# Three of the four weight sums of a Strassen pair made by accumulating DMAs instead of VectorE

## The chip, the cores and the metric

The kernel runs on one core of a Trainium2 chip. The metric is the device time of one execution in microseconds (us). The runs shown are 2701.43, 2702.08 and 2699.49 us (median 2701.43); besides them one execution was recorded by the profiler. Engines are named as the profile names them: PE is TensorE, DVE is VectorE, ACT is ScalarE, POOL is GpSimd, SP is SyncE. All DMAs of the kernel before are issued by SP.

## The reference

Two layers of one trunk work on 512 latent and 256 context tokens of width 2048, in float32. Each layer normalises and modulates the tokens, multiplies them with one wide input matrix, runs four groups of attention heads, and multiplies the gated result with an output matrix. In the last layer the context tokens are needed only as keys and values.

```python
for l in range(DEPTH):                       # DEPTH = 2
    with_ctx = l < DEPTH - 1
    shift, scale, gate = jnp.split(silu_c @ w_mod[l] + b_mod[l], 3, axis=-1)
    n = rms_norm(h, pre_norm_g[l]) * (1.0 + scale[:, None]) + shift[:, None]
    nc = rms_norm(hc, pre_norm_g[l]) * (1.0 + scale_c) + shift_c
    p = jnp.split(n @ w_in[l], split_points, axis=-1)      # w_in[l]: 2048 x 7168
    pc = jnp.split(nc @ w_in[l], split_points, axis=-1)
    ...                                                    # four attention groups oa, ob, on, od
    y = (jnp.concatenate([oa, ob, on, od], axis=-1) * jax.nn.silu(p[12])) @ w_out[l]
    h = h + gate[:, None] * rms_norm(y, post_norm_g[l])
```

The change touches only the product with `w_in`.

## The kernel before

**Numbers as pairs.** A float32 matrix is held as a high part in `fp32r` and a low part with the rest. One product is three matmuls: high times high, high times low, low times high (`mm3`, L301 to L303). `split` makes the two parts: ACT copies the high part (L292), then DVE subtracts it from the source (L293). Split weights lie in the tiles `wh` and `wl`, four buffers each, so a split waits until PE is done with the product four before.

**The Strassen stage.** The 56 column blocks of `w_in` (128 columns each) are taken in 28 pairs per layer. For the first half of the 2048 input channels a pair is a 2 by 2 matrix of quarters (512 channels x 128 columns, 256 KB) times a 2 by 2 matrix of token blocks; it is done in seven products instead of eight. The four quarters of a pair are loaded by SP into `wr` (L211, six buffers); `g[0]` and `g[3]` are the two quarters of the first column block, `g[1]` and `g[2]` those of the second. Four sums of quarters are needed, and DVE makes all of them: L166 makes `s1 = g1 + g2`, L167 makes `s2 = s1 - g0`, L168 makes `g0 - g1` in place in `g[1]`, and L179 makes `g3 - s2` in place in `g[3]`. `s1` and `s2` lie in two buffers, tag `wsum`. The seven products run in the order 1, 6, 2, 5, 7, 3, 4 (in the first pair of a layer 1, 2, 6, 5, 7, 3, 4); product 6 takes `s2`, product 5 takes `s1`, product 7 takes the sum in `g[1]` and product 3 the sum in `g[3]`.

**Banks.** Products 1 and 2 gather in one PSUM bank, products 6, 5 and 3 in a second, products 7 and 4 in a third. After each product ACT or DVE reads its bank: 1 and 2 by ACT (L777, L781), 6, 5 and 3 by DVE with the copy `s` of product 1 (L784, `c<-ps,s`), 7 and 4 by DVE onto what stands in `c` (L784, `c<-ps,c`). PE may not go on in a bank that is not read yet: product 3 waits for the read of 5, product 4 for the read of 7. When products 3 and 4 are read, `c` is stored to `part` (L787).

**Wide and narrow.** In layer 0 every product has 384 moving columns (512 latent and 256 context tokens in two halves). In layer 1 the pairs of keys and values have 384 (12 pairs, called wide below), those of queries and gates 256 (16 pairs, narrow).

**Order.** `weight()` is called before each product and first calls `weights_ahead()`, which issues the splits up to two products ahead and all loads for which a buffer is free; the sums of a pair are issued after the split for product 3 of the pair before. During the stage the step list `late` puts columns of the modulation (`w_mod`) beside the products: loads `mraw` (L426) and DVE's L443. The order of the instructions on an engine is set when the kernel is built, by a scheduler that goes by data dependences, and each engine runs its own list strictly in that order.

**Between the layers.** `out_phase` ends layer 0 with the residual (L1442), the norm of the next layer and its transposes (`token_half`, L559), and `reload` makes the token operands of products 1 to 7 (splits into `arena`) from `token_sums` (L570 to L575). The first weight sums of layer 1 are made there too. The second half of the input channels is done later, block by block, in the attention stage, and is not touched.

Of the kernel before, what the change touches and what calls it, by code (L numbers as in the profile page):

```python
# [10 lines left out]
F32 = mybir.dt.float32  # L11
# [3 lines left out]
ALU = mybir.AluOpType  # L15
# [3 lines left out]
P = 128  # L19
# [63 lines left out]
class Kernel:  # L83
# [35 lines left out]


    def push_pair(self, l, s, b1, b2, order):
        g = {"sums": False}
        for i, (b, c) in enumerate(((b1, 2 * s), (b2, 2 * s), (b2, 2 * s + 1), (b1, 2 * s + 1))):
            self.lq.append((g, i, ("in", (l, b, c))))
        self.wq += [("st", g, n) for n in order]

    def push_one(self, kind, key):
# [25 lines left out]
    def new_pair(self):  # L153
# [2 lines left out]
        self.ws[self.wsplit] = hi, lo  # L156
        return hi, lo

    def sums(self, g):

        if g["sums"] or not all(self.need(g, i) for i in range(3)):
            return g["sums"]
        add = self.nc.vector
        g["s1"] = self.wp.tile([P, 512], F32, tag="wsum", bufs=2, name="s1")
        g["s2"] = self.wp.tile([P, 512], F32, tag="wsum", bufs=2, name="s2")
        add.tensor_add(g["s1"], g[1], g[2])  # L166
        add.tensor_sub(g["s2"], g["s1"], g[0])  # L167
        add.tensor_sub(g[1], g[0], g[1])  # L168
        g["sums"] = True
        return True  # L170

    def split_product(self, g, n):
        if not all(self.need(g, i) for i in {1: (0,), 2: (3,)}.get(n, ())) or not self.sums(g):
            return False
        src = {1: 0, 6: "s2", 2: 3, 5: "s1", 7: 1, 3: 3, 4: 2}[n]
        hi, lo = self.new_pair()
        self.split(hi, lo, g[src])
        if n == 2:
            self.nc.vector.tensor_sub(g[3], g[3], g["s2"])  # L179
        elif src in (0, 1, 2, 3):  # L180
            self.retire(g, src)
        if n == 3:
            for kind, other, m in self.wq[self.wsplit + 2:self.wsplit + 3]:
                if kind == "st":
                    self.sums(other)
        return True
# [14 lines left out]
    def load_one(self):  # L201
        nc, a = self.nc, self.a
        if self.live >= self.raws or self.wload >= len(self.lq):
            return False
        g, i, (kind, key) = self.lq[self.wload]
        if kind == "og" and key not in self.stored:
            return False
        raw = self.wp.tile([P, 512], F32, tag="wr", bufs=RAWS, name="wr")
        if kind == "in":
            l, b, c = key  # L210
            nc.sync.dma_start(raw, a["w_in"][l, b, :, 4 * c:4 * c + 4, :].rearrange("p k c -> p (k c)"))  # L211
        elif kind == "out":
            l, k, c = key
            nc.sync.dma_start(raw, a["w_out"][l, k * P:(k + 1) * P, c * 512:(c + 1) * 512])
        else:
            l, s, k = key
            w0, w = ((0, SEQ), (SEQ, CTX))[s]
            raw = raw[:, 0:w]
            nc.sync.dma_start(raw, self.ogd[l, k, :, w0:w0 + w])
        g[i] = raw  # L220
        self.live += 1
        self.wload += 1
        return True
# [227 lines left out]
    def mod_finish(self, job, accs, fold=True):  # L451

        nc = self.nc
        l, kind, c4, streams = job
        ns = len(streams)
        if not fold or ns == 1:
            ps = self.tbank()
            for j in range(4):
                for i in range(ns):
                    nc.tensor.matmul(ps[:, ns * j + i:ns * j + i + 1], accs[i][:, j * P:(j + 1) * P], self.ones[:, 0:1], start=True, stop=True)  # L460
            self.mod_columns(l, kind, c4, ps[:, 0:4 * ns].rearrange("p (j s) -> p j s", s=ns))
            return
        if ns == 2:
            t, col = self.mp.tile([P, 512], F32, tag="mt", bufs=2, name="fold"), self.halves
            a, b = slice(0, 64), slice(64, P)
            nc.scalar.activation(t[a], accs[0][b], AF.Copy)
            nc.scalar.activation(t[b], accs[1][a], AF.Copy)
            nc.vector.tensor_add(t[a], t[a], accs[0][a])
            nc.vector.tensor_add(t[b], t[b], accs[1][b])

        def sums():
            ps = self.tbank()
            for j in range(4):
                nc.tensor.matmul(ps[:, ns * j:ns * j + ns], t[:, j * P:(j + 1) * P], col, start=True, stop=True)
            self.mod_columns(l, kind, c4, ps[:, 0:4 * ns].rearrange("p (j s) -> p j s", s=ns))

        self.later(2, sums)
# [83 lines left out]
    def token_sums(self, ns, ts, what):  # L561


        add = self.nc.vector

        def step(j):
            (b11, b12), (b21, b22) = ns[j], ns[4 + j]
            x, y = ts[j]
            if what == 1:
                add.tensor_sub(x, b12, b11)  # L570
                add.tensor_sub(y, b22, x)
            elif what == 4:
                add.tensor_sub(y, b21, y)
            else:
                add.tensor_sub(x, b22, b12)  # L575

        return [lambda j=j: step(j) for j in range(4)]

    def reload(self, n, ns, ts):

        hi, lo = self.operand(n)

        def step(j):
            if n in (1, 2, 3):
                src = ns[j + (0 if n == 1 else 4)][int(n == 3)]
            else:
                src = ts[j][{5: 0, 7: 0, 6: 1, 4: 1}[n]]
            self.split(hi[:, j], lo[:, j], src)

        return [lambda j=j: step(j) for j in range(4)]  # L590

# [155 lines left out]
    def pair_slots(self, l, n, i, order, hooks=None):  # L747

        nc = self.nc
        blocks = self.units[n][3][i]  # L750
        wide = l < DEPTH - 1 or blocks[0][0] == "k"
        w = HT if wide else 2 * P
        before, after = hooks or ({}, {})
        r = {}

        def slot(m, half):
            if half == 0:
                for fn in before.get(m, ()):
                    fn()
                r["w"] = self.weight()  # L760
            hi, lo = r["w"]
            th, tl = self.operand(m)
            out = self.bank(CHAIN[m], w)
            for j in (2 * half, 2 * half + 1):
                js = slice(j * P, (j + 1) * P)
                self.anchors[1] = self.mm3(out, hi[:, js], lo[:, js], th[:, j, 0:w], tl[:, j, 0:w], m in FIRST and j == 0, m in LAST and j == 3, True)
            if half:
                read(m, out)
                for fn in after.get(m, ()):
                    fn()  # L770

        def read(m, ps):
            V = nc.vector
            if m == 1:
                r["c"] = [self.cp.tile([P, 2, HT], F32, tag="c", bufs=4, name="c")[:, :, 0:w] for _ in blocks]
                r["s"] = self.cp.tile([P, HT], F32, tag="s", bufs=1, name="s")[:, 0:w]
                nc.scalar.activation(r["s"], ps, AF.Copy)  # L777
                return
            c1, c2 = r["c"]
            if m == 2:  # L780
                nc.scalar.activation(c1[:, 0], ps, AF.Copy)  # L781
            else:
                c = {6: c2[:, 0], 4: c2[:, 0], 5: c2[:, 1], 7: c2[:, 1], 3: c1[:, 1]}[m]
                self.anchors[0] = V.tensor_add(c, ps, c if m in (7, 4) else r["s"])  # L784
            if m in (3, 4):
                c, (_, b) = (c1, blocks[0]) if m == 3 else (c2, blocks[1])
                nc.sync.dma_start(self.part[l, b, :, :, 0:w], c)  # L787

        return [lambda m=m, half=half: slot(m, half) for m in order for half in range(2)]
# [94 lines left out]
    def qk_block(self, l, b, kind, is_q, dst):  # L884
# [33 lines left out]
        def norm_part(c, sl, part):  # L918
# [31 lines left out]
            def scale(dg):  # L950
# [3 lines left out]
                self.split_to(dst, sl, x)  # L954

            self.later(4, sums)

        return done
# [654 lines left out]
```

## Time and profile before

| what | before |
|---|---|
| median of the runs | 2701.43 us |
| profiled execution, its own time | 2703.73 us |
| its span, first to last instruction | 2701.6 us |
| mean granted TensorE clock | 0.984 |
| busy: PE, DVE, ACT, POOL | 96%, 81%, 48%, 2% |
| Strassen stage of layer 0, of layer 1 | about 90 to 510 us, about 1580 to 1917 us |
| DMAs issued by POOL | none |

A line of the profile's windows gives, for a stretch of the span, the busy time of each engine with the number of its instructions in brackets, the granted clock as a share of full speed, the share of time in which the 16 DMA engines were busy, and what they moved. A line of a group of instructions ends with the busy time and the mean length in ns, and after a second bar the idle time of that engine just before these instructions, with what ended it. A timeline row gives start and length in us, engine, line, operation and tiles, and in square brackets the idle time before it. Matmuls are pipelined, so their busy time overlaps itself; the step from one to the next is read from their number in a window.

### The profile page before, as it was taken

Reading aid. Unit: us, or ns where it says so; the run is one execution under the profiler, and the core shown is the slowest. Engines: PE = TensorE matmul, PEld = TensorE weight load, DVE = VectorE, ACT = ScalarE, POOL = GpSimd, SP = SyncE. Lnnn points to the kernel's source line nnn. Section 1 sums busy time; section 2 is a strip of 40 time slices with the busy share of each in tenths; the row PEclk is TensorE's granted clock in tenths of the full one; section 3 lists DMA queues with packets and bytes.
Section 4 is the critical chain, followed back from the end, with each engine's and each line's share of the span. In section 5 each row is a group of like instructions: output and inputs, shape, how many; then the busy total and the mean of one; then the engine's idle time right before and its main releaser. Section 6 shows DMA issues by size and latency. Waiting matters only on the chain.

```text
span 2701.6 us, 41385 instructions
## 1 busy us (share of the span) xinstructions
PE 2591.7 (96%) x14392; PEld 2231.2 (83%) x14392; DVE 2187.2 (81%) x4480; ACT 1285.7 (48%) x2532; POOL 43.6 (2%) x42
## 2 busy tenths in 40 slices
PE   7899999999999999999999689999999999999997
PEld 1799999987888888887777479999878887888885
DVE  4899998789899888767889989887798988876524
ACT  3534343445556455546533464444455554544422
POOL 0000000000000000000010000000000000000001
PEclk9899999999999999999999789999999999999998
DMA  9455554422223334427886535444422334444632
GB/s 318 138 197 194 196 196 149 151 73 78 85 96 116 119 126 142 140 89 232 293 269 218 201 123 170 148 146 137 152 87 86 112 121 136 146 154 129 223 103 98
DMA packets 230497, 411.09 MB, mean 152 GB/s; under 512 B 25568, under 2 KB 59664, under 8 KB 229776
## 3 DMA queue, kind: packets, MB, share of 16 engines
q1 hardware_dynamic: 230288, 408.45, 46.3%
q8 instruction: 113, 1.85, 0.3%
q14 instruction: 96, 0.79, 0.1%
HBM read 348.17 MB, written 60.19 MB: 151 GB/s over the span
## 4 chain that ended last, share of the span: by engine, by line
PE 76%; DVE 11%; DMA 7%; ACT 3%; issue 2%; SPq 0%; POOL 0%; DVEq 0%; ACTq 0%; POOLq 0%
PE ps L301 23%; PE ps L302 23%; PE ps L303 22%; DMA mraw<-in_w_mod 3%; PE ps L1132 3%; DVE macc L443 2%; DVE wl L293 1%; PE ps L650 1%; PE ps L1034 1%; DMA mr<-in_w_mod 1%; DVE rt L862 1%; DVE h L1442 1%; PE ps L1035 1%; DMA wr<-in_w_out 1%; DMA wr<-ogd 1%
## 5 line engine op out<-in xcount | busy, mean ns | idle before, releaser
L301 PE MATMUL ps<-arena,wh 128*128 128x384 f32 (+2 forms) x3104 | 1050.6, 339 | 16.6 <-ACT arena L292 7.4
L302 PE MATMUL ps<-arena,wh 128*128 128x384 f32 (+2 forms) x3104 | 1038.8, 335 | 0.0
L303 PE MATMUL ps<-arena,wl 128*128 128x384 f32 (+2 forms) x3104 | 1037.7, 335 | 0.0
L292 ACT ACTIVATE wh<-wr 128x512 fp32r<-128x512 f32 x696 | 437.8, 630 | 710.1 <-PE ps L302 371.3
L301 PEld LDWEIGHTS ps<-arena,wh 128*128 128x128 f32 x3104 | 586.9, 189 | 47.5 <-ACT arena L292 8.6
L293 DVE TENSOR_TENSOR wl<-wr,wh 128x512 fp32r<-128x512 f32 x696 | 477.4, 688 | 176.3 <-ACT wh L292 163.7
L303 PEld LDWEIGHTS ps<-arena,wl 128*128 128x128 f32 x3104 | 587.0, 189 | 33.0
L302 PEld LDWEIGHTS ps<-arena,wh 128*128 128x128 f32 x3104 | 587.8, 189 | 27.4 <-DVE arena L293 1.1
L443 DVE SCALAR_TENSOR_TENSOR macc<-mraw,sc,macc 128x512 f32<-128x512 f32 x540 | 391.2, 750 | 38.3 <-DMA mraw<-in_w_mod 37.6
L302 PE MATMUL ps<-wl,arena 128*128 128x512 f32 x640 | 255.6, 399 | 9.2 <-DVE wl L293 9.1
L303 PE MATMUL ps<-wh,arena 128*128 128x512 f32 x640 | 253.0, 395 | 0.0
L301 PE MATMUL ps<-wh,arena 128*128 128x512 f32 x640 | 248.2, 397 | 0.0
L292 ACT ACTIVATE PTh<-ps 128x512 fp32r<-128x512 f32 (+2 forms) x224 | 114.2, 519 | 123.0 <-PE ps L1132 117.6
L293 DVE TENSOR_TENSOR PTl<-ps,PTh 128x512 fp32r<-128x512 f32 (+2 forms) x224 | 130.7, 591 | 34.1 <-ACT PTh L292 32.6
L302 PEld LDWEIGHTS ps<-wl,arena 128*128 128x128 f32 x640 | 120.4, 188 | 45.4 <-DVE wl L293 18.3
L303 PEld LDWEIGHTS ps<-wh,arena 128*128 128x128 f32 x640 | 120.4, 188 | 28.0
L301 PEld LDWEIGHTS ps<-wh,arena 128*128 128x128 f32 x640 | 120.2, 188 | 28.0 <-DVE c L819 0.2
L292 ACT ACTIVATE wh<-s 128x512 fp32r<-128x512 f32 x112 | 70.8, 633 | 135.2 <-PE ps L302 96.9
L1132 PE MATMUL ps<-ident,P 128*128 128x128 f32 x672 | 112.6, 274 | 2.0 <-DVE P L1069 0.7
L784 DVE TENSOR_TENSOR c<-ps,s 128x384 f32<-128x384 f32 (+1 forms) x168 | 86.5, 515 | 33.2 <-PE ps L303 24.6
L1132 PEld LDWEIGHTS ps<-ident,P 128*128 128x128 f32 x672 | 83.9, 140 | 32.3 <-ACT P L1111 5.3
L1111 ACT ACTIVATE P<-P,small 128x768 f32<-128x768 f32 (+2 forms) x96 | 79.4, 827 | 44.9 <-DVE small L1110 44.6
(262 smaller groups left out, 3196.7 us busy)
## 6 DMA issues: line engine op xcount, KB each, us to landing
wr<-in_w_in SPq DMA_DIRECT2D x448, 256.0 KB, 3.2
mraw<-in_w_mod SPq DMA_DIRECT2D x320, 256.0 KB, 3.0
wr<-in_w_out SPq DMA_DIRECT2D x192, 256.0 KB, 3.5
part<-c SPq DMA_DIRECT2D x80, 384.0 KB, 2.6
c<-part SPq DMA_DIRECT2D x80, 384.0 KB, 3.1
mr<-in_w_mod SPq DMA_DIRECT2D x32, 512.0 KB, 5.3
part<-c SPq DMA_DIRECT2D x32, 256.0 KB, 3.0
c<-part SPq DMA_DIRECT2D x32, 256.0 KB, 3.1
```

The source lines that it names most:

```text
L292: nc.scalar.activation(hi, src, AF.Copy)
L293: nc.vector.tensor_sub(lo, src, hi.bitcast(F32))
L301: mm(out, lh, rh, start=start, stop=False, skip_group_check=parts)
L302: mm(out, lh, rl, start=False, stop=False, skip_group_check=parts)
L303: return mm(out, ll, rh, start=False, stop=stop, skip_group_check=parts)
L443: nc.vector.scalar_tensor_tensor(acc, raw, col, acc, op0=ALU.mult, op1=ALU.add)
L650: nc.tensor.matmul(self.ps[0:2, 2 * c4 + 1 - kind, :], self.sc[:, k, :], raw, start=k == 0, stop=k == KT - 1)
L784: self.anchors[0] = V.tensor_add(c, ps, c if m in (7, 4) else r["s"])
L862: nc.vector.tensor_mul(fit(t2[o:o + hw], x), x[i:i + hw], fit(sin[i:i + hw], x))
L1034: self.nc.tensor.matmul(out, q["hd"[sub]][:, qs], kt[:, ks], start=True, stop=False)
L1111: nc.scalar.activation(Pt, Pt, AF.Copy, scale=sm)
L1132: nc.tensor.transpose(T[:, i * P:(i + 1) * P], st["P", t][:, c:c + P], self.ident)
```

## The change

Three of the four sums are made by DMAs that add to what lies in the destination (`accum_op=ALU.add`), issued from POOL. `s1` gets its own tile: SP loads `g1`'s quarter into it a second time, then POOL adds `g2`'s quarter from memory. The tile of `g[1]` is loaded by SP and POOL adds `g0`'s quarter. `s2 = s1 + g0` stays on DVE (L180 of the changed kernel); after its split for product 6 POOL adds `g3`'s quarter to it, and product 3 takes it from there. Since a DMA only adds, the quarters `g0` and `g3` enter with the other sign, and the token sums, one token operand (`reload`, scale -1 for product 3) and the reads of the banks are turned to match.

```diff
+    def add_quarter(self, t, key):
+
+        self.nc.gpsimd.dma_start(t, self.quarter(key), accum_op=ALU.add)
+
+    def first_sum(self, g):
+
+        if "s1" not in g:
+            g["s1"] = self.wp.tile([P, 512], F32, tag="wsum", bufs=2, name="s1")
+            self.nc.sync.dma_start(g["s1"], self.quarter(g["keys"][1]))
+            self.add_quarter(g["s1"], g["keys"][2])
+
     def sums(self, g):
...
-        add = self.nc.vector
-        g["s1"] = self.wp.tile([P, 512], F32, tag="wsum", bufs=2, name="s1")
+        self.first_sum(g)
         g["s2"] = self.wp.tile([P, 512], F32, tag="wsum", bufs=2, name="s2")
-        add.tensor_add(g["s1"], g[1], g[2])
-        add.tensor_sub(g["s2"], g["s1"], g[0])
-        add.tensor_sub(g[1], g[0], g[1])
+        self.nc.vector.tensor_add(g["s2"], g["s1"], g[0])
...
-        src = {1: 0, 6: "s2", 2: 3, 5: "s1", 7: 1, 3: 3, 4: 2}[n]
+        src = {1: 0, 6: "s2", 2: 3, 5: "s1", 7: 1, 3: "s2", 4: 2}[n]
         hi, lo = self.new_pair()
         self.split(hi, lo, g[src])
-        if n == 2:
-            self.nc.vector.tensor_sub(g[3], g[3], g["s2"])
+        if n == 6:
+            self.add_quarter(g["s2"], g["keys"][3])
         elif src in (0, 1, 2, 3):
             self.retire(g, src)
+        if n == 5:
+            for kind, other, m in self.wq[self.wsplit + 4:self.wsplit + 5]:
+                if kind == "st":
+                    self.first_sum(other)
...
-            nc.sync.dma_start(raw, a["w_in"][l, b, :, 4 * c:4 * c + 4, :].rearrange("p k c -> p (k c)"))
+            nc.sync.dma_start(raw, self.quarter(key))
+            if i == 1:
+                self.add_quarter(raw, g["keys"][0])
...
-                add.tensor_sub(x, b22, b12)
+                add.tensor_sub(x, b12, b22)
...
-            self.split(hi[:, j], lo[:, j], src)
+            self.split(hi[:, j], lo[:, j], src, -1.0 if n == 3 else None)
```

In a scaled split DVE's instruction is a `scalar_tensor_tensor` instead of a `tensor_tensor` (four per layer). The reads of 6, 5 and 3 become subtractions (L805), the reads of 7 and 4 stay additions (L802).

DVE in layer 1, one narrow pair (its reads have 256 columns) with no modulation steps beside it, from the split for product 5 on. `wl<-s1` is that split; the reads are `c<-ps,s` and `c<-ps,c`. Before:

```order
L293 TENSOR_TENSOR wl_17263<-s1_17160,wh_17262 128x512
L168 TENSOR_TENSOR wr_17188<-wr_17165,wr_17188 128x512
L293 TENSOR_TENSOR wl_17284<-wr_17042,wh_17283 128x512
L167 TENSOR_TENSOR s2_17307<-s1_17306,wr_17165 128x512
L784 TENSOR_TENSOR c_17259<-ps_72,s_17260 128x256
L293 TENSOR_TENSOR wl_17303<-wr_17141,wh_17302 128x512
L293 TENSOR_TENSOR wl_17327<-wr_17065,wh_17326 128x512
L784 TENSOR_TENSOR c_17259<-ps_72,s_17260 128x256
L293 TENSOR_TENSOR wl_17346<-wr_17165,wh_17345 128x512
L784 TENSOR_TENSOR c_17259<-ps_72,c_17259 128x256
```

The same pair after:

```order
L310 TENSOR_TENSOR wl_17304<-s1_17164,wh_17303 128x512
L310 TENSOR_TENSOR wl_17328<-wr_17079,wh_17327 128x512
L805 TENSOR_TENSOR c_17300<-ps_72,s_17301 128x256
L310 TENSOR_TENSOR wl_17347<-s2_17203,wh_17346 128x512
L310 TENSOR_TENSOR wl_17366<-wr_17103,wh_17365 128x512
L805 TENSOR_TENSOR c_17300<-ps_72,s_17301 128x256
L310 TENSOR_TENSOR wl_17386<-wr_17184,wh_17385 128x512
L180 TENSOR_TENSOR s2_17350<-s1_17307,wr_17184 128x512
L802 TENSOR_TENSOR c_17300<-ps_72,c_17300 128x256
```

L166, L168 and L179 are gone; the sum that is left, `s2` of the next pair (L180), moved from ahead of the read of product 6 to directly ahead of the read of product 7, and its source `s1_17307` now comes from DMAs. In most wide pairs L180 stands earlier, directly ahead of the read of product 5.

SP around the same place; `part<-c_17157` stores the pair before, `s1_17307` is the source of the sum above. Before:

```order
L787 DMA part_96<-c_17116 128x768
L787 DMA part_96<-c_17117 128x768
L211 DMA wr_17287<-in_w_in 128x512
L211 DMA wr_17311<-in_w_in 128x512
L211 DMA wr_17330<-in_w_in 128x512
```

After:

```order
L808 DMA part_96<-c_17156 128x768
L226 DMA wr_17285<-in_w_in 128x512
L808 DMA part_96<-c_17157 128x768
L171 DMA s1_17307<-in_w_in 128x512
L226 DMA wr_17331<-in_w_in 128x512
L226 DMA wr_17369<-in_w_in 128x512
```

The load of `s1` stands behind the second store and ahead of the loads of the pair after next; it may start when the split for product 5 (`wl_17304<-s1_17164` above) has freed its buffer. POOL's list, empty of DMAs before, has three per pair there:

```order
L165 DMA s1_17307<-in_w_in 128x512
L165 DMA wr_17369<-in_w_in 128x512
L165 DMA s2_17350<-in_w_in 128x512
L165 DMA s1_17454<-in_w_in 128x512
L165 DMA wr_17512<-in_w_in 128x512
```

DVE between the layers, ahead of the residual (L1442 before, L1463 after), where a chain of small instructions makes a reciprocal root (`rs`, `small`). Before:

```order
L1431 TENSOR_REDUCE s1_15702<-ss_14394 128x2
L167 TENSOR_TENSOR s2_15839<-s1_15838,wr_15471 128x512
L514 TENSOR_TENSOR small_15633<-rs_15626 128x2
L168 TENSOR_TENSOR wr_15498<-wr_15471,wr_15498 128x512
L515 SCALAR_TENSOR_TENSOR small_15633<-small_15633,small_15631 128x2
L293 TENSOR_TENSOR wl_15844<-wr_15471,wh_15843 128x512
L516 SCALAR_TENSOR_TENSOR rs_15626<-small_15633,rs_15626 128x2
L293 TENSOR_TENSOR wl_15848<-wr_15546,wh_15847 128x512
L514 TENSOR_TENSOR small_15633<-rs_15626 128x2
L293 TENSOR_TENSOR wl_15853<-s2_15839,wh_15852 128x512
L515 SCALAR_TENSOR_TENSOR small_15633<-small_15633,small_15631 128x2
L179 TENSOR_TENSOR wr_15546<-wr_15546,s2_15839 128x512
```

After:

```order
L1452 TENSOR_REDUCE s1_15732<-ss_14422 128x2
L310 TENSOR_TENSOR wl_15874<-wr_15499,wh_15873 128x512
L531 TENSOR_TENSOR small_15663<-rs_15656 128x2
L310 TENSOR_TENSOR wl_15878<-wr_15575,wh_15877 128x512
L532 SCALAR_TENSOR_TENSOR small_15663<-small_15663,small_15661 128x2
L310 TENSOR_TENSOR wl_15882<-s2_15871,wh_15881 128x512
L533 SCALAR_TENSOR_TENSOR rs_15656<-small_15663,rs_15656 128x2
L310 TENSOR_TENSOR wl_15907<-s1_15868,wh_15906 128x512
L531 TENSOR_TENSOR small_15663<-rs_15656 128x2
L532 SCALAR_TENSOR_TENSOR small_15663<-small_15663,small_15661 128x2
L533 SCALAR_TENSOR_TENSOR rs_15656<-small_15663,rs_15656 128x2
```

The three large sums between the small steps are gone from there; L180 of this pair moved ahead of the reads of the last output bank, and the last three small steps follow one another with nothing between.

More of the change, by code (lines that the diff above doesn't have):

```diff
@@ L121, in push_pair @@
     def push_pair(self, l, s, b1, b2, order):
-        g = {"sums": False}
-        for i, (b, c) in enumerate(((b1, 2 * s), (b2, 2 * s), (b2, 2 * s + 1), (b1, 2 * s + 1))):
-            self.lq.append((g, i, ("in", (l, b, c))))
+        g = {"sums": False, "keys": [(l, b1, 2 * s), (l, b2, 2 * s), (l, b2, 2 * s + 1), (l, b1, 2 * s + 1)]}
+        for i, key in enumerate(g["keys"]):
+            self.lq.append((g, i, ("in", key)))
         self.wq += [("st", g, n) for n in order]
@@ L157, in new_pair, with quarter @@
         return hi, lo
+    def quarter(self, key):
+        l, b, c = key
+        return self.a["w_in"][l, b, :, 4 * c:4 * c + 4, :].rearrange("p k c -> p (k c)")
+    def add_quarter(self, t, key):
[5 more added lines that the diff above has]
+            self.add_quarter(g["s1"], g["keys"][2])
     def sums(self, g):
@@ L209, in load_one @@
         if kind == "in":
-            l, b, c = key
-            nc.sync.dma_start(raw, a["w_in"][l, b, :, 4 * c:4 * c + 4, :].rearrange("p k c -> p (k c)"))
+            nc.sync.dma_start(raw, self.quarter(key))
+            if i == 1:
+                self.add_quarter(raw, g["keys"][0])
         elif kind == "out":
@@ L783, in read @@
                 c = {6: c2[:, 0], 4: c2[:, 0], 5: c2[:, 1], 7: c2[:, 1], 3: c1[:, 1]}[m]
-                self.anchors[0] = V.tensor_add(c, ps, c if m in (7, 4) else r["s"])
+                if m in (7, 4):
+                    self.anchors[0] = V.tensor_add(c, ps, c)
+                else:
+                    x, y = (r["s"], ps) if m == 3 else (ps, r["s"])
+                    self.anchors[0] = V.tensor_sub(c, x, y)
             if m in (3, 4):
```

## The prediction

> **What bounds the kernel now.** First the page's busy times, then windows inside the Strassen stage, then PE's waits there, then the chain at the stage's two ends.
>
> ```profile
> span 2701.6 us, 41385 instructions
> PE 2591.7 (96%) x14392; PEld 2231.2 (83%) x14392; DVE 2187.2 (81%) x4480; ACT 1285.7 (48%) x2532; POOL 43.6 (2%) x42
> ...
> 200.00:250.00 50.00, 50.00 (x291) 50.00 (x290) 49.71 (x84) 19.16 (x34) 0.00 (x0) 1.00 0.61 200
> 450.00:500.00 50.00, 50.00 (x293) 50.00 (x292) 33.89 (x62) 21.16 (x39) 0.00 (x0) 1.00 0.37 129
> ...
> PE ps L301 <- DVE c L784: 0.2, 1, 0.2
> ...
> PE ps L301 <- DVE c L784: 1.6, 2, 1.4
> ```
>
> The two windows lie in layer 0. DVE is busy 49.71 of 50 us in the one (modulation steps beside the products) and 33.89 in the other, and PE does 291 and 293 matmuls: it keeps its step of 50 / 293 = 0.171 us whether DVE is full or not. The two last rows are all that PE waits for DVE between 130 and 500 us and between 1580 and 1925 us: 1.8 us. So the weight sums, though DVE works on them, cost the stage next to nothing, and what the change can win in it is below 2 us. What it can win lies at the ends of the stage, where PE has not started and DVE's list is the path:
>
> ```profile
> 79.48 0.61 DVE s L167
> ...
> 98.79 0.60 DVE s L167
> 99.39 0.60 DVE wr L168
> ...
> 114.30 0.60 DVE s L166
> ...
> 115.37 0.60 DVE s L167
> 115.97 0.60 DVE wr L168
> ...
> 1525.46 0.60 DVE s L167
> 1526.13 0.60 DVE wr L168
> ...
> 1528.82 0.60 DVE wr L179
> ...
> 1535.40 0.61 DVE s L166
> 1536.03 0.69 DVE s L167
> 1536.80 0.60 DVE wr L168
> ```
>
> These rows of the chain that ended last, in order of time, have start and length in us; the sums among them stand between other DVE steps that follow at once.
>
> **What is removed.** Per pair three DVE sums go, 168 in all:
>
> ```profile
> L166 DVE TENSOR_TENSOR s<-wr 128x512 f32<-128x512 f32 x56 | 38.4, 685 | 0.9 <-DMA wr<-in_w_in 0.5
> L443 DVE SCALAR_TENSOR_TENSOR macc<-mraw,sc,macc 128x512 f32<-128x512 f32 x540 | 391.2, 750 | 38.3 <-DMA mraw<-in_w_mod 37.6
> ```
>
> 168 x 0.685 = 115 us less of DVE, of which I count only what lies on the chain. At the start L168, L166 and L168 go: 3 x 0.6 = 1.8 us; one L167 per pair stays as L180. Between the layers L168, L179, L166 and L168 go, 2.4 us, and L167 at 1536.03 (0.69) moves behind the residual. The small steps of the reciprocal root stood between those sums; three of them now follow each other bare, and the reduction after 1536 still waits for ACT, so I take 2.5 us of the 3.1, and give 0.6 back where L180 comes later, on DVE's path before the first reads of layer 1. The scaled split of product 3's operand is a scalar_tensor_tensor: by the two rows above 0.065 us more on 512 columns, 0.05 on 384, eight times: 0.4 us. Ends: -1.8 - 2.5 + 0.6 + 0.4 = -3.3 us. Reads as subtractions cost what additions cost.
>
> **What is added, and who waits.** SP gets one issue per pair, POOL three. SP's load of `s1` waits for DVE's split for 5, and behind it on SP stand loads of the pair after next and of `w_mod` two steps ahead: their lead hides the wait and the 0.33 us of the issue (row below); without it each would be that much late. POOL's list waits for the landing of each load before it adds; behind the `s1` add stand the one into `g[1]`, made a pair ahead, and the one into `s2`, which has from the split for 6 to the split for 3, four products (4 x 1.41 = 5.6 us in narrow pairs). Both are covered up to about 5 us; beyond that the split for 3 is late. The one that is not covered is `s1`: its buffer comes free at the split for product 5, and L180, which reads it, stands two splits later in DVE's strict order, with the read that PE needs behind it.
>
> ```profile
> 1776.25 0.42 DVE L784 TENSOR_TENSOR c<-ps,c 128x256 f32<-128x256 f32 x1 [0.18 <-PE ps L303]
> ...
> 1777.66 0.42 DVE L784 TENSOR_TENSOR c<-ps,s 128x256 f32<-128x256 f32 x1
> ...
> 1779.54 0.41 DVE L784 TENSOR_TENSOR c<-ps,c 128x256 f32<-128x256 f32 x1
> 1779.88 0.68 DVE L293 TENSOR_TENSOR wl<-s,wh 128x512 fp32r<-128x512 f32 x1
> 1780.47 0.68 DVE L166 TENSOR_TENSOR s<-wr 128x512 f32<-128x512 f32 x1
> ...
> 1794.11 0.55 DVE L784 TENSOR_TENSOR c<-ps,c 128x384 f32<-128x384 f32 x1
> ```
>
> ```profile
> L292 ACT ACTIVATE wh<-wr 128x512 fp32r<-128x512 f32 x125 | 79.1, 633 | 110.2 <-PE ps L302 80.5 <-issue 12.4 <-DVE wl L293 8.0
> ...
> L211 SPq DMA_DIRECT2D wr<-in_w_in x68: 327/328/778, 1702.6 to 1899.5; - x68
> ...
> DMA to landing us min/median/max: 3.0/3.1/3.6
> ```
>
> The first fence is DVE's timeline, the end of a narrow pair and one read of a wide one: the reads of 7 and 3 start 1.41 us apart, which is a narrow product; a wide one is 12 x 0.171 = 2.05. Full-width DVE steps that follow at once start 0.6 apart (1779.88, 1780.47). The second has ACT's high part, which waits mostly for PE, and the loads of quarters between 1700 and 1900 us, with issue in ns and landing in us. Call 0 the moment PE starts a pair. Then the buffers of the product four before come free: ACT's high part 0.63, DVE's low part 0.69, 0.1 for handing on: the split for 5 ends at 1.4. SP loads `s1`, 3.1: landed at 4.5. POOL's adding DMA takes A. L180 costs 0.6, the read 0.4 narrow, 0.55 wide, handing on 0.1.
> - Narrow: L180 stands ahead of the read of 7, and PE needs that at product 4, at 6 x 1.41 = 8.46. Stall = 4.5 + A + 1.1 - 8.46 = A - 2.85, say A - 2.8. 13 pairs stand so in the list (of 15 with a successor, two of the early ones have L180 later).
> - Wide: L180 stands ahead of the read of 5, needed at product 3, at 5 x 2.05 = 10.25. Stall = 4.5 + A + 1.25 - 10.25 = A - 4.5. 29 pairs. Three in layer 0 have a modulation step (0.75) between: A - 3.8; three in layer 1 a split between: A - 3.9.
>
> A stall is not won back: PE does nothing but products there, and the next pair repeats it.
>
> **How large is A.** No DMA of the trace adds and none is issued by POOL. The nearest rows are SP's:
>
> ```profile
> wr<-in_w_in SPq DMA_DIRECT2D x448, 256.0 KB, 3.2
> h<-h SPq DMA_DIRECT2D x16, 256.0 KB, 6.8
> cst<-in_rope_sub SPq DMA_DIRECT2D x2, 512.0 KB, 4.2
> cst<-in_rope_head SPq DMA_DIRECT2D x2, 512.0 KB, 3.5
> n<-cnd SPq DMA_DIRECT2D x16, 64.0 KB, 1.8
> ```
>
> From below 1.8 us (64 KB), from above 6.8 (the slowest 256 KB). An adding DMA reads the destination beside the source, so 512 KB move: 3.5 to 4.2 us. I take 4.0, near the upper of these since descriptors by POOL are in no row. The Trainium skill ("DMA: Bandwidth & Descriptors", section "Anatomy of one DMA — SWDGE (gpsimd) path") fits a plain DMA issued from GpSimd with 2.0 us plus bytes over 436 GB/s, an estimate of 2.6 us for 256 KB; by it no pair would stall and the sum would be -3.3. The trace's own SP loads of that size take 3.2, longer than the fit, and no run here shows a DMA of POOL, so I stay with the rows.
>
> At A = 4.0: narrow 13 x 1.2 = 15.6, the three with a step 0.6, the three with a split 0.3, other wide 0: +16.5. Sum +16.5 - 3.3 = +13.2. The profiled execution took 2703.7 us, 2.3 over the median of the runs, so 2716.9 there and **2714.6** as a median. At A = 1.8 it is 2698.1; at 6.8 narrow 52, wide 66.7, the others 17.7: 2834.
>
> **Rivals.** 0.2% (5.4 us) is about what runs of this kernel can tell from no change.
> *Covered.* A below 2.8, L180 never waits: -3.3 us, 2698.1, no change. For it: the minimum of SP's loads is 3.0, and a rule of the skill gives 2.6. Against it: software descriptors and a second stream.
>
> *Faster.* As before, and at both ends every sum leaves the path: the five start rows (3.0) and the five between the layers (3.1), with L167 at 79.48 and 1525.46 gone too (1.2), less 0.4 for the scaled splits: -6.9, 2694.5. It decides once the ends give over 5.4. Against it: ACT's work stands beside, and L180 still runs once per pair.
>
> *Slow adder.* A above 4.5, so the wide pairs stall too. At 5.7: narrow 37.7, wide 34.8, the six others 11.1: +83.6 - 3.3, 2782. For it: h<-h 6.8 shows such landings, where several DMAs are queued together; three adding DMAs share POOL's list.
>
> *DMA engines full*, the last rival: beside the modulation steps they are busy 0.61 (window from 200 us).
>
>
> ```profile
> q1 hardware_dynamic: 230288, 408.45, 46.3%
> ...
> DMA to landing us min/median/max: 2.9/3.3/4.3
> ```
>
> The first row is the queue of all DMAs, the second the landing of quarters between 150 and 450 us. 46.3% of 2701.6 are 1250.8 us for 408 MB, 0.80 us for a quarter. One more load and three adding ones per pair of 14.35 us make 4 x 0.8 = 3.2 us (0.83), or 5.6 (1.00) if an adding one costs double. Then loads land late, say twice 3.3 us: 2.8 us in each of some 17 pairs, +48 us, 2760. The skill's section "Issuing engines are not separate DMA queues" on the same page says that all issuers share the 16 engines; the trace has one issuer only and cannot show it.
>
> **How the numbers follow.** The forecast (A from 3.5 to 4.5, 2707 to 2724) gets 0.42; covered 0.18, faster 0.12, slow adder 0.15, engines full 0.08; 0.05 for a loss below 5.4 us. Slower is 0.42 + 0.15 + 0.08 = 0.65, same 0.18 + 0.05 = 0.23, faster 0.12. The range takes in half of faster and slow adders to A = 5.7: 2695 to 2780.
>
> **What would show it.** DVE idle before L180 with a DMA of `s1` as its end, over 1 us in narrow pairs, near 0 in wide ones; PE waiting for DVE's read of 7 in layer 1 (13 times about 1.2 us), while 150 to 500 us stays at 291 to 293 matmuls per 50 us; adding DMAs landing in about 4 us; DVE's busy time 115 us lower; layer 1's first product some 3 us earlier relative to the stage ahead. Wrong would be: landings under 3 us, waits in wide pairs, or `mraw` late in layer 0. The granted clock should stay at 1.00, as in the windows above.

## The result

| | before | after |
|---|---|---|
| median of the runs, us | 2700.46 (4 runs) | 2954.26 (4 runs, 2951.11 to 2960.34) |
| span of the profiled execution, us | 2701.6 | 2953.7 |
| mean granted TensorE clock | 0.984 | 0.957 |

The ratio is 1.0944, 95% interval 1.0923 to 1.0965: 9.4% slower, far above the forecast 2714.6 and its range. The page of the changed kernel begins:

```profile
span 2953.7 us, 41772 instructions
PE 2674.6 (91%) x14392; PEld 2298.2 (78%) x14392; DVE 2096.0 (71%) x4312; ACT 1279.7 (43%) x2532; POOL 189.8 (6%) x210
...
q1 hardware_dynamic: 238352, 423.14, 44.1%
q0 software_dynamic: 24192, 44.05, 9.1%
```

DVE works 91 us less, and PE does the same 14392 matmuls. PE's idle time (span less busy) went from 109.9 to 279.1 us, +169.2; its busy time rose by 82.9, although it does the same work. The granted clock is of that size: 2953.7 x 0.043 = 127 us are lost to it, 43 before, +84. 169 + 83 = 252, which is the whole difference of the spans. So the question is where PE stands still, and why its clock fell.

Windows of the changed kernel, the first two as they were shown of before, the third in layer 1:

```profile
200.00:250.00 50.00, 40.49 (x216) 39.62 (x215) 35.72 (x63) 13.67 (x24) 6.97 (x8) 0.93 0.75 207
450.00:500.00 50.00, 45.37 (x253) 44.50 (x252) 22.54 (x39) 19.60 (x34) 7.79 (x9) 0.97 0.66 171
1900.00:1950.00 50.00, 40.73 (x260) 40.03 (x260) 23.01 (x42) 16.73 (x31) 7.79 (x9) 0.90 0.67 164
```

216 and 253 matmuls stand where 291 and 293 stood. DVE is idle in 29 to 55% of these stretches, so it isn't short of time; it waits. Who waits for whom in the whole execution (total us, times, longest):

```profile
PE ps L318 <- DVE c L805: 119.2, 44, 7.0
PE ps L318 <- DVE c L802: 43.3, 15, 4.0
DVE s L180 <- DMA s<-in_w_in: 150.6, 42, 5.1
ACT wh L309 <- DMA s<-in_w_in: 68.5, 23, 7.1
```

PE waits 162 us for reads of banks, DVE 151 us in front of L180 for `s1`, and ACT 69 us for the other sum that DMAs make, `s2`. The DMAs of the changed kernel (KB, median us from issue to landing):

```profile
s<-in_w_in POOLq DMA_DIRECT2D x112, 256.0 KB, 4.9
s<-in_w_in SPq DMA_DIRECT2D x56, 256.0 KB, 4.6
wr<-in_w_in POOLq DMA_DIRECT2D x56, 256.0 KB, 4.3
part<-c SPq DMA_DIRECT2D x80, 384.0 KB, 4.4
```

The store to `part` took 2.6 us before. One narrow pair of layer 1, from the timeline, first DVE and the two queues, then PE:

```profile
1857.88 0.69 DVE L310 TENSOR_TENSOR wl<-s,wh 128x512 fp32r<-128x512 f32 x1
...
1858.60 0.33 SPq L171 DMA_DIRECT2D s<-in_w_in  x1
...
1863.35 0.86 POOL L165 DMA_DIRECT2D s<-in_w_in  x1 [9.22 <-DVE wl L310]
...
1868.06 0.69 DVE L180 TENSOR_TENSOR s<-s,wr 128x512 f32<-128x512 f32 x1 [3.83 <-DMA s<-in_w_in]
1868.66 0.42 DVE L802 TENSOR_TENSOR c<-ps,c 128x256 f32<-128x256 f32 x1
```

```profile
1865.50 0.28 PE L320 MATMUL ps<-arena,wl 128*128 128x256 f32 x1
1869.23 0.55 PE L318 MATMUL ps<-arena,wh 128*128 128x256 f32 x1 [3.45 <-DVE c L802]
1869.58 0.41 PE L319 MATMUL ps<-arena,wh 128*128 128x256 f32 x1
1869.79 0.41 PE L320 MATMUL ps<-arena,wl 128*128 128x256 f32 x1
```

The low part of the split for 5 ends at 1858.57 and frees the buffer; SP loads, POOL adds 4.75 us later, L180 starts 4.71 us after that, and PE resumes behind the read that stands after L180. Then matmuls that had a step of 0.118 us (1.41 / 12) go with 0.21: the record of the granted clock has 0.5 here for 6.8 us, called half clock below. Over the pairs of layer 0, from SP's load to POOL's add 5.5 us pass (median) and from there to the landing 4.8; in layer 1 5.7 and 4.4. Nearly every pair has a stall: 75.6 us in 25 pairs of layer 0, 72.4 in 24 of layer 1, 3.0 each.

### The profile page after: what moved, and what is told of

The parts are those of the page before. It is cut to its first block, busy times and chain, and to the rows that moved or that the text cites. A ratio compares the mean times of both kernels' runs of the same rounds, so it can differ in the third digit from the quotient of the medians.

```text
span 2953.7 us, 41772 instructions
## 1 busy us (share of the span) xinstructions
PE 2674.6 (91%) x14392; PEld 2298.2 (78%) x14392; DVE 2096.0 (71%) x4312; ACT 1279.7 (43%) x2532; POOL 189.8 (6%) x210
## 4 chain that ended last, share of the span: by engine, by line
PE 51%; DMA 13%; DVE 12%; issue 4%; ACT 4%; POOL 0%; SPq 0%; DVEq 0%; ACTq 0%; POOLq 0%
PE ps L318 16%; PE ps L319 15%; PE ps L320 15%; DMA s<-in_w_in 7%; DMA mraw<-in_w_mod 3%; DVE wl L310 2%; DVE macc L460 2%; PE ps L1153 2%; DMA wr<-in_w_in 2%; ACT wh L309 1%; DMA wr<-ogd 1%; PE ps L1055 1%; DVE rt L883 1%; PE ps L1056 1%; DVE h L1463 1%
## 5 line engine op out<-in xcount | busy, mean ns | idle before, releaser
L318 PE MATMUL ps<-arena,wh 128*128 128x384 f32 (+2 forms) x3104 | 1083.6, 349 | 183.0 <-DVE c L805 119.2
L319 PE MATMUL ps<-arena,wh 128*128 128x384 f32 (+2 forms) x3104 | 1065.8, 343 | 4.4 <-DVE arena L310 4.4
L320 PE MATMUL ps<-arena,wl 128*128 128x384 f32 (+2 forms) x3104 | 1064.7, 343 | 0.1
L318 PEld LDWEIGHTS ps<-arena,wh 128*128 128x128 f32 x3104 | 610.0, 197 | 228.5 <-issue 149.6
L309 ACT ACTIVATE wh<-wr 128x512 fp32r<-128x512 f32 x640 | 401.8, 629 | 683.5 <-PE ps L319 372.4
L319 PEld LDWEIGHTS ps<-arena,wh 128*128 128x128 f32 x3104 | 611.1, 197 | 32.2 <-DVE arena L310 5.8
L320 PEld LDWEIGHTS ps<-arena,wl 128*128 128x128 f32 x3104 | 609.9, 197 | 33.5 <-DVE wl L310 0.4
L310 DVE TENSOR_TENSOR wl<-wr,wh 128x512 fp32r<-128x512 f32 x640 | 440.3, 690 | 222.9 <-ACT wh L309 213.9
L309 ACT ACTIVATE wh<-s 128x512 fp32r<-128x512 f32 x168 | 106.1, 631 | 403.4 <-DVE s L180 205.5
L180 DVE TENSOR_TENSOR s<-s,wr 128x512 f32<-128x512 f32 x56 | 38.7, 692 | 190.4 <-DMA s<-in_w_in 150.6
L310 DVE TENSOR_TENSOR wl<-s,wh 128x512 fp32r<-128x512 f32 x168 | 115.5, 688 | 49.8 <-ACT wh L309 48.1
L165 POOL DMA_DIRECT2D s<-in_w_in x112 | 98.9, 883 | 606.7 <-DVE wl L310 307.5
```

Source lines behind the costliest of these rows:

```text
L165: self.nc.gpsimd.dma_start(t, self.quarter(key), accum_op=ALU.add)
L180: self.nc.vector.tensor_add(g["s2"], g["s1"], g[0])
L309: nc.scalar.activation(hi, src, AF.Copy)
L310: nc.vector.tensor_sub(lo, src, hi.bitcast(F32))
L318: mm(out, lh, rh, start=start, stop=False, skip_group_check=parts)
L319: mm(out, lh, rl, start=False, stop=False, skip_group_check=parts)
```

## The experiments

Two theories stood at first. A: the chain of `s1` alone makes the loss. B: the adding DMAs harm by their traffic. Each loss is against the runs of before on the same chip (medians 2702.9, 2701.1 and 2705.0 us for the first, second and third four). The kernels differ in length, so the lines shown of them can be numbered a few off those of the changed kernel (L180 is L181 in one, for example).

**Only `s1` by DMA.** The two other sums go back to DVE.

```diff
+        self.nc.vector.tensor_add(g[1], g[0], g[1])
...
-        src = {1: 0, 6: "s2", 2: 3, 5: "s1", 7: 1, 3: "s2", 4: 2}[n]
+        src = {1: 0, 6: "s2", 2: 3, 5: "s1", 7: 1, 3: 3, 4: 2}[n]
...
-        if n == 6:
-            self.add_quarter(g["s2"], g["keys"][3])
+        if n == 2:
+            self.nc.vector.tensor_add(g[3], g[3], g["s2"])
...
-            if i == 1:
-                self.add_quarter(raw, g["keys"][0])
```

> One of the three sums stays with the DMAs: s1 (load, then adding DMA), made and read as in the changed kernel; the sums into g[1] and for product 3 are DVE's again (168 - 56 = 112 DVE sums, 56 adding DMAs in place of 168, 15 MB less traffic for each of the two). Theory A, the chain of s1: the loss of 254 us is PE's wait for s1 at one place per pair (about 167 us of stalls, 53 of them, 3.0 us each) and the half clock that follows a stall (about 82 us); the chain is still there, one or two tenths of a us shorter where POOL's list is emptier: 2900 to 2950 us, and 45 or more waits of PE for a read. Theory B, the adding DMAs themselves (traffic, DMA engines, POOL's descriptors) slow all that is loaded: two thirds of them are gone, so two thirds of the loss, about 2785 us.

Measured 2918.4 us, ratio 1.0794 (1.0768 to 1.0820): +216. The one adding DMA per pair that is left has POOL to itself, lands in 5.2 us, and DVE waits longer for it than in the changed kernel (151 us there):

```profile
DVE s L180 <- DMA s<-in_w_in: 207.7, 54, 6.0
```

So the chain of `s1` alone does most of it, and two thirds of the adding DMAs fewer help little. That fits A. It is not the whole:

**All but `s1` by DMA.**

```diff
-        self.first_sum(g)
...
-        self.nc.vector.tensor_add(g["s2"], g["s1"], g[0])
+        self.nc.vector.tensor_add(g["s2"], g[1], g[2])
+        self.nc.vector.tensor_sub(g["s1"], g["s2"], g[0])
...
-        if n == 5:
...
-                    self.first_sum(other)
```

> The other way about: s1 is DVE's, the two other sums stay with adding DMAs. With k0 already in g[1] DVE makes s2 = g[1] + g[2] and s1 = s2 - g[0], both from loaded quarters; 112 adding DMAs are left. Theory A: no wait is left that PE sees, 2690 to 2706 us, fewer than 5 waits of PE for a read in the two stages, granted clock back at 0.98. Theory B: a third of the loss goes, about 2870 us.

Measured 2812.6, ratio 1.0412 (1.0396 to 1.0427): +110, where A had said none and B a third of the loss.

**All DMAs kept, L180 without `s1`.**

```diff
-        self.nc.vector.tensor_add(g["s2"], g["s1"], g[0])
+        self.nc.vector.tensor_add(g["s2"], g[1], g[2])
```

> The changed kernel with one operand pair exchanged: s2 = g[1] + g[2] (k0 is already in g[1], so the value is the same) in place of s1 + g[0]. All 168 adding DMAs, the extra load and the traffic stay; s1 is still loaded and added to by DMA, but the first that reads it is the split for product 5, four products later. Theory A: the stalls go with the dependence: 2690 to 2710 us. Theory B: nothing is taken away from the DMAs: about 2950 us. A value between says how much of each.

Measured 2859.6, ratio 1.0570 (1.0544 to 1.0596): +157. With every adding DMA in place 97 us are won back by one operand, but both theories missed. The waits of these two kernels, first the former, then the latter, name a second chain:

```profile
ACT wh L306 <- DMA s<-in_w_in: 183.7, 45, 7.3
```

```profile
ACT wh L309 <- DMA s<-in_w_in: 223.2, 51, 9.8
```

It is ACT's split for product 3, which waits for the DMA that adds into `s2`. In the former (DMA rows) the two adders land so:

```profile
wr<-in_w_in POOLq DMA_DIRECT2D x56, 256.0 KB, 5.8
s<-in_w_in POOLq DMA_DIRECT2D x56, 256.0 KB, 7.6
```

The timeline of the latter shows one:

```profile
1851.86 0.88 POOL L165 DMA_DIRECT2D wr<-in_w_in  x1 [3.00 <-DVE c L805]
1852.46 1.16 POOL L165 DMA_DIRECT2D s<-in_w_in  x1
...
1860.15 0.63 ACT L309 ACTIVATE wh<-s 128x512 fp32r<-128x512 f32 x1 [5.08 <-DMA s<-in_w_in]
...
1860.82 0.69 DVE L310 TENSOR_TENSOR wl<-s,wh 128x512 fp32r<-128x512 f32 x1 [4.64 <-ACT wh L309]
...
1861.54 0.69 DVE L180 TENSOR_TENSOR s<-wr 128x512 f32<-128x512 f32 x1
...
1862.15 0.68 DVE L310 TENSOR_TENSOR wl<-wr,wh 128x512 fp32r<-128x512 f32 x1
...
1862.76 0.42 DVE L805 TENSOR_TENSOR c<-ps,s 128x256 f32<-128x256 f32 x1
```

POOL issues the add into the next pair's `g[1]` and 0.6 us later the one into `s2`, which is usable only 7.7 us after its issue. ACT's and DVE's lists stand behind that split, and with them the read that PE needs. In this kernel 50 of the 56 adds into `s2` were issued within 1.5 us of another (and one into `s1`); the median landing of these is 8.2 us, and 4.3 that of the 53 adds into sums with 6 us of distance.

**The sum later in DVE's list.** The sum is issued behind the read of 3; `g[0]`'s buffer is kept until then.

```diff
+        with self.tc.issue_after(self.anchors[0].ins) if self.anchors[0] else ExitStack():
+            self.nc.vector.tensor_add(g["s2"], g["s1"], g[0])
...
+        if "one" in g:
+            self.retire(g, 0)
...
-        if not all(self.need(g, i) for i in {1: (0,), 2: (3,)}.get(n, ())) or not self.sums(g):
+        if not all(self.need(g, i) for i in {1: (0,), 2: (3,)}.get(n, ())) or n != 1 and not self.sums(g):
...
-        if n == 3:
-            for kind, other, m in self.wq[self.wsplit + 2:self.wsplit + 3]:
-                if kind == "st":
-                    self.sums(other)
```

> The changed kernel, its sum s2 = s1 + g[0] unchanged, but moved in DVE's list behind the read of product 3 (in the changed kernel it stands ahead of the read of 5 or of 7, which PE waits for); g[0]'s buffer is kept until then. From split for 5 to the sum the chain takes about 9.8 us (load 4.5, POOL 0.7, adding DMA 4.5), so s1 is there 11.2 us after PE starts the pair. The next pair's second product starts at 8 products and wants sum and split 2.0 us before. Theory A: wide pairs (8 x 2.05 = 16.4) wait for nothing, narrow ones (8 x 1.41 = 11.3) 2.0 us each, 13 times, mostly too short for the half clock: 2715 to 2745 us. Theory B: 2950 us. If the half clock had another cause than the stalls (the DMAs' own activity), 82 us of loss stay: about 2800.

Measured 2928.3, ratio 1.0828 (1.0809 to 1.0847): +225, a miss. DVE hardly waits for `s1` any more; ACT does, at two places:

```profile
ACT wh L310 <- DMA s<-in_w_in: 286.9, 50, 7.2
ACT wh L310 <- DVE s L181: 262.1, 51, 8.7
```

The later sum makes a later split for 6, a later add into `s2`, and so a later split for 3. I had looked at the read behind the sum and not at what the sum feeds.

**One adder alone: `g[1]`, then `s2`.** In the first `s2` and `s1` are made as in the kernel with all but `s1`, and product 3's sum by DVE; in the second DVE makes all but the add into `s2`.

```diff
-        self.nc.vector.tensor_add(g["s2"], g["s1"], g[0])
+        self.nc.vector.tensor_add(g["s2"], g[1], g[2])
+        self.nc.vector.tensor_sub(g["s1"], g["s2"], g[0])
...
-        if n == 6:
-            self.add_quarter(g["s2"], g["keys"][3])
+        if n == 2:
+            self.nc.vector.tensor_add(g[3], g[3], g["s2"])
...
```

> One adding DMA per pair is left, the one that adds k0 into g[1] right behind its load; s2 = g[1] + g[2], s1 = s2 - g[0] and the sum for product 3 are DVE's. With the two adders of g[1] and s2 together 110 us were lost (2812.6). Theory A, each adder costs by how late its own result is, and the s2 one was late because it stood right behind the g[1] one on POOL (landing 7.8 us when issued within 1.5 us of another, 4.3 when alone): here nothing stands in front, the landing is 4.3 to 5.7 us, and only what PE waits for the sum where g[1] comes late remains: 2700 to 2730 us. Theory B, every adding DMA costs a share of its own by its traffic: half of 110, about 2755 us.

```diff
+        self.nc.vector.tensor_add(g["s1"], g[1], g[2])
         self.nc.vector.tensor_add(g["s2"], g["s1"], g[0])
+        self.nc.vector.tensor_add(g[1], g[0], g[1])
...
-            if i == 1:
-                self.add_quarter(raw, g["keys"][0])
```

> One adding DMA per pair is left, the one that adds k3 into s2 after the split for 6; s1, s2 and the sum in g[1] are DVE's as before. Theory A: alone on POOL it lands in about 4.5 us; issued 1.0 us before PE starts product 1 of the pair's... place of the split for 5, it leaves 5.0 us in narrow pairs before the read of 5 is late and about 9 in wide ones: almost no stall, 2698 to 2715 us. Theory B: half of 110, about 2755 us.

`g[1]` alone: 2756.8, 1.0193 (1.0165 to 1.0221), +56. That is B's number, but the trace shows a wait: L180 reads `g[1]` in this kernel (the changed kernel reads it only at the split for 7), and in 47 of the 56 pairs it starts within 0.15 us of the landing. `s2` alone: 2717.2, 1.0052 (1.0035 to 1.0069), +16, against +55 by B. The DMA is of the same kind and size in both; what differs is how soon the result is needed. Together they cost 110, more than 56 + 16; there the one stands behind the other, which the run on the order below bears out.

**Writing instead of adding.** The accumulation is taken off the three DMAs, so the weights lack the sums.

```diff
-        self.nc.gpsimd.dma_start(t, self.quarter(key), accum_op=ALU.add)
+        self.nc.gpsimd.dma_start(t, self.quarter(key))
```

> All three GpSimd DMAs of a pair stay where they are with the same bytes, but write instead of adding, so the weights are not the sums. It prices the addition against the issue by software. If reading the destination back is what makes a landing 4.3 us and more (SP's plain load of the same 256 KB takes 3.2), the landings fall to about 2.6 to 3.2, the chain of s1 ends 1.5 us earlier, and stalls fall from 3.0 to about 1.5 us, mostly without the half clock: 2780 to 2830 us. If the issue by software costs it, landings stay at 4.3 to 4.9 and the time at 2950.

Measured 2848.8, ratio 1.0549 (1.0521 to 1.0578): +148. The landings:

```profile
s<-in_w_in POOLq DMA_DIRECT2D x112, 256.0 KB, 3.9
wr<-in_w_in POOLq DMA_DIRECT2D x56, 256.0 KB, 3.8
```

With 6 us to the issue before, landings into `s` are 3.5 us (least 3.1) against 4.5 (least 4.1) in the changed kernel: adding costs 1.0 us. The issue itself is shorter too: POOL takes 0.54 us for a plain one, 0.87 for an adding one. Without the addition the loss is 106 us smaller; each of the three chains has such a landing. The time came out above the range I gave: PE is still idle 97 us longer than in the kernel before.

**The order on POOL.** The kernel in which L180 reads `g[1]` and `g[2]`, with the add into the next `g[1]` put off to the split for 5, behind the add into `s2`.

```diff
...
+            with self.tc.issue_after(self.third.ins) if self.third else ExitStack():
+                self.add_quarter(g[1], g["keys"][0])
...
+            self.third = self.add_quarter(g["s2"], g["keys"][3])
```

> The kernel with s2 = g[1] + g[2] (2859.6 us), all 168 adding DMAs kept, but the one into the next pair's g[1] is put on POOL's list behind the one into s2 in place of right ahead of it. There 51 of the 56 adds into s2 were issued within 1.5 us of another and landed in 8.2 us, and ACT's split for 3 waited 223 us for them. Theory A, an adding DMA that follows another at once waits for it: the adds into s2 land in 4.3 to 5 us, ACT's wait falls below 80 us, and the time to 2740 to 2790 us. Theory B, three adding DMAs a pair are more than the software queue or the 16 engines carry, in whatever order: 2840 us or more.

Measured 2778.3, ratio 1.0281 (1.0258 to 1.0305): +77 in place of +157, with every DMA kept. ACT's wait falls to 90 us, and the landings change places:

```profile
s<-in_w_in POOLq DMA_DIRECT2D x112, 256.0 KB, 5.4
wr<-in_w_in POOLq DMA_DIRECT2D x56, 256.0 KB, 7.8
```

The one that follows another at once is the late one, whichever it is. Theory B can't be the whole: the same bytes, half the loss. What of the 77 us that are left is traffic isn't shown.

**The sums left out: what could be won at all.**

```diff
-        add.tensor_add(g["s1"], g[1], g[2])
-        add.tensor_sub(g["s2"], g["s1"], g[0])
-        add.tensor_sub(g[1], g[0], g[1])
+        add.tensor_sub(g["s2"], g[1], g[0])
...
-        src = {1: 0, 6: "s2", 2: 3, 5: "s1", 7: 1, 3: 3, 4: 2}[n]
+        src = {1: 0, 6: "s2", 2: 3, 5: "s2", 7: 1, 3: 3, 4: 2}[n]
...
-            self.nc.vector.tensor_sub(g[3], g[3], g["s2"])
```

> The kernel before with three of the four sums of a pair left out and nothing put in their place: s2 = g[1] - g[0] alone is made, the splits for 5, 7 and 3 read what is there (products of wrong weights, the same work otherwise). 168 DVE sums, 115 us of DVE, are gone at no price. It bounds what any way of moving these sums off DVE can win. If DVE's sums lie on no path but at the ends of the stage, as the windows of before say (1.8 us of PE's waits inside), 2692 to 2701 us, 0 to 0.35% faster; if DVE's load costs PE more than its waits show, 2600 to 2680.

Measured 2701.7 against 2705.0, ratio 0.9988 (0.9977 to 0.9998), with 94 us of DVE gone:

```profile
PE 2586.7 (96%) x14392; PEld 2229.1 (83%) x14392; DVE 2092.8 (78%) x4312; ACT 1285.0 (48%) x2532; POOL 42.9 (2%) x42
```

At no price at all the change would win 3 us, at most 6 by the interval. That bounds what any way of moving these three sums off DVE can win in this order of the lists.

**`s1` with lead.** The kernel with only `s1` by DMA, a third `wsum` buffer, five `wr` buffers, the load issued three products earlier and the sum behind the read of 7.

```diff
-RAWS = 6
+RAWS = 5
...
-            g["s1"] = self.wp.tile([P, 512], F32, tag="wsum", bufs=2, name="s1")
+            g["s1"] = self.wp.tile([P, 512], F32, tag="wsum", bufs=3, name="s1")
...
+        with self.tc.issue_after(self.anchors[0].ins) if self.anchors[0] else ExitStack():
+            self.nc.vector.tensor_add(g["s2"], g["s1"], g[0])
...
-        if n == 5:
-            for kind, other, m in self.wq[self.wsplit + 4:self.wsplit + 5]:
+        if n == 1:
+            for kind, other, m in self.wq[self.wsplit + 7:self.wsplit + 8]:
...
```

> The kernel with s1 alone made by DMA (2918 us), but with lead: a third buffer for the sums, so that the load and the adding DMA of s1 are issued at the split for product 1 of the pair before (seven products before the first split of its own pair) and not at the split for 5, and the sum s2 in DVE's list behind the read of 7. One buffer of loaded quarters is given up for it (5 in place of 6). Same DMAs, same bytes. If lateness alone made the 216 us, it takes what the kernel before takes with 5 such buffers, within 10 us; if adding DMAs harm by being there, 2800 us or more.

Its control is the kernel before with that one edit to `RAWS`:

> The kernel before with 5 buffers of loaded quarters in place of 6, to compare with the run on early s1. Loads of quarters took 3.1 to 3.2 us and a product takes 1.41 or 2.05, so one buffer less leaves a lead of some four products: 2700 to 2715 us.

Measured 2732.2 (1.0095, 1.0077 to 1.0113) and 2727.3 (1.0083, 1.0065 to 1.0100). The intervals overlap: the 216 us of the `s1` chain are gone, though its adding DMA lands as late after its issue as before:

```profile
s<-in_w_in POOLq DMA_DIRECT2D x56, 256.0 KB, 5.2
```

So lateness was the cost. The run changes two things that could end it, the start of the chain and the place of the sum. Its trace speaks for the first: in 54 pairs `s1` had landed at least 0.6 us (one sum) ahead of the read of 7 in 52, and ahead of the read of 5 in 46, so in most pairs it would have been in time for the sum's old place too. Neither was run alone. The missing `wr` buffer costs 22 us by itself, more than I expected of it.

**Stalls without DMAs.** DVE makes the sum into `s1` nine times in the kernel before.

```diff
+        for _ in range(9):
+            add.tensor_add(g["s1"], g[1], g[2])
```

> The kernel before, no DMA changed, with the sum into s1 made nine times over (the same values): 8 x 0.6 = 4.8 us more of DVE per pair. In some 25 pairs beside modulation steps DVE is full, and PE waits about 4.8 us there; elsewhere DVE has 4.6 us of slack per pair and PE waits 0 to 2. It tells whether the half clock belongs to stalls of PE or to the DMAs. If to stalls: waits of 3 us and more are followed by 3.4 us or more at half clock as in the changed kernel (97 of 102 such waits in nine profiles with adding DMAs, 2 of 121 under 1.5 us), and the time is about 2830 to 2890. If to the DMAs: the granted clock stays at 0.98 and the time is 2790 to 2840.

Measured 2903.2, ratio 1.0734 (1.0707 to 1.0761), a little above the range. The clock falls with no DMA changed. PE in the timeline:

```profile
1821.68 0.34 PE L304 MATMUL ps<-arena,wl 128*128 128x384 f32 x1
1826.23 0.45 PE L302 MATMUL ps<-arena,wh 128*128 128x384 f32 x1 [4.21 <-ACT wh L293]
...
1828.18 0.52 PE L303 MATMUL ps<-arena,wh 128*128 128x384 f32 x1
1828.50 0.52 PE L304 MATMUL ps<-arena,wl 128*128 128x384 f32 x1
...
1830.27 0.34 PE L304 MATMUL ps<-arena,wl 128*128 128x384 f32 x1
1830.44 0.34 PE L303 MATMUL ps<-arena,wh 128*128 128x384 f32 x1
```

After 4.21 us of waiting the step is 0.32 us instead of 0.17 for 3.4 us. All 7 of this run's waits of 3 us and more that had no other wait in the 5 us ahead of them are followed by such a stretch. So the half clock belongs to the stall, whatever causes it. Of this run's 73 us more of busy PE the clock (0.971) makes 41; the rest I can't explain.

## Why the prediction was wrong

**Right:** the mechanism and its place. DVE waits before L180 for `s1`, a read behind L180 is late, PE stands still, and nothing is won back. Inside the stage the sums cost nothing before (1.8 us), as the run with the sums left out shows.

**Wrong, the chain of `s1`.** The step "SP loads `s1`, 3.1: landed at 4.5. POOL's adding DMA takes A" took the load's landing from a stretch without adding DMAs and passed from the landing to the add in no time. From load to add it took 5.5 to 5.7 us in place of 3.1: the load 4.6 by its median row (3.4 in the kernel with only `s1` by DMA), and 0.67 us from landing to POOL's issue. The adding DMA landed in 4.4 to 4.8 for A = 4.0. From the split to L180 that is some 10.5 us where 7.1 was forecast. The largest part falls on a term that I had set to 0: the wide pairs, with A - 4.5 = -0.5, wait 3.0 us each, which the prediction had named as a sign against it. The sum of stalls, +16.5, is 148 us in the 49 pairs that were measured.

**Wrong, "the granted clock should stay at 1.00".** A stall was priced at its own length. Half of the time again came on top: 83 us for 169 of waiting.

**Wrong, "Both are covered up to about 5 us".** The adds into `s2` and `g[1]` were each taken as alone on POOL's queue. Alone, `s2` costs 16 us; issued right behind the other it lands in 7 to 8 us. How much of the 254 us is this chain's can't be told, since its waits lie beside those of `s1`: 216 and 110 alone make 326.

**Wrong, the ends, -3.3.** PE's first product of the stage starts at 81.7 us instead of 78.4, and from layer 0's last product of this kind to layer 1's first pass 344.9 us instead of 343.6: 4.6 lost. The size wasn't far off: in the run with the sums left out, PE gains 0.6 us on the kernel before up to matmul 160 of layer 0's stage and 3.4 us up to matmul 60 of layer 1's (one profile of each). In the changed kernel nothing of it is left; that what takes the sums' place waits for DMAs is the likely cause, and no run shows it for the ends alone.

**Wrong, "DVE's busy time 115 us lower".** It fell by 91 us, and by 94 in the run with the sums left out. The mean of 0.685 counts the overlap with the next step, which starts 0.60 later; that makes 14 us of it, and the rest is open.

**The rivals.** Slow adder pointed the right way, but with A = 5.7 and nothing else in the chain. Engines full is not it: their busy share did rise (0.75 in the first window above, 0.61 before), and loads of quarters in the stage that overlapped one adding DMA landed in a median of 4.3 us, against 3.2 in the kernel before; but the run with lead stands 4.9 us from its control, with the adding DMAs of `s1`, a third of all, still there. The traffic's part is that it makes the links of the chains longer. The Trainium skill ("DMA: Bandwidth & Descriptors", section "Anatomy of one DMA — SWDGE (gpsimd) path") gives an estimate of 2.6 us for such a plain transfer. By that rule the forecast would have been lower still. The trace of the plain writes has 3.1 at the least and 3.5 in the middle with POOL free, from the start of an issue of 0.54, and adding comes on top.

## What to carry to other kernels

Moving work off an engine that PE does not wait for wins nothing: first leave the work out and see what is there to win. Before a step is made by a DMA, add up every link from what frees the buffer to the first reader (load, hand-over, adding DMA, the reader's place in its engine's strict list), with landings taken under the new traffic, and give it a buffer more if that is longer than the lead. Price a repeated stall of PE above about 2 us at its length and about half again.

## What the runs showed of the hardware

- **The clock after a stall.** Over ten profiles, counting waits of PE inside the two stages, away from their ends, with 5 us of no wait before them: of 149 waits under 1.5 us 4 were followed by half clock, of 40 from 1.5 to 2 us 10, of 77 from 2 to 3 us 38, of 109 from 3 us on 104. In the records of the clock most of these stretches last 3.4 us; after waits of 3 us and more about a third last 6.8, and after waits over 5 us 9 of 10. A part of the long ones lies in the wait itself: by size of the wait, 3.8 to 4.9 us at half clock are left on average when PE resumes, which is some 2 us of work. The Trainium skill ("TensorE: Matmul & The Clock Gate", section "Part 1: The HAM clock gate (the "warmup" mystery)") tells of a free-running window of 3.4 us and of the low state after at least one idle window; the stretches agree, but here waits of 2 us were enough half the time.
- **Adding DMAs of 256 KB from POOL.** Each takes POOL 0.87 us (a plain one 0.54). With 6 us to the issue before, the least landing is 4.1 us (plain ones 3.1), and the median lies between 4.3 and 6.1 by kernel and sum. What else is under way goes with it: over 499 such adds of eight kernels it is 4.2 us where other DMAs moved less than 200 KB around the first 4 us, and 6.3 where they moved over 900 KB; how busy DVE was makes little difference (4.6 to 5.2). Issued within 1.5 us of another, the median is 7.0 us in the changed kernel (9 cases), 7.8 in the one with all but `s1` by DMA (49) and 8.2 in the one with all DMAs and L180 without `s1` (51). The Trainium skill ("DMA: Bandwidth & Descriptors", section "SWDGE vs HWDGE vs iDMA") names a single software queue; the landings fit that, and no run here tests it.
